# First stage of a two-layer diffusion backbone: adaLN scale and shift made one feature tile at a time

## The chip, the cores and the metric

The kernel runs on one core of a Trainium2 chip. Five engines work beside one another, each through its own instructions in order: TensorE (PE, with its weight loads PEld), VectorE (DVE), ScalarE (ACT), GpSimd (POOL) and SyncE (SP), whose queue issues most of the loads; 16 DMA engines move the data. The metric is the time of one execution on the device in microseconds, as the median of several runs.

## What is computed

The reference is one inference step of two trunk layers over 640 tokens (512 latent and 128 context tokens) of width 1024. Layer 0 mixes with latent attention and neighbourhood attention, layer 1 with grouped-query attention; each is followed by a SwiGLU network. What the change touches is the head of layer 0: the modulation vectors, the first norm and the first projection.

```python
def rms_norm(x, g):
    xf = x.astype(jnp.float32)
    y = xf * lax.rsqrt(jnp.mean(xf * xf, axis=-1, keepdims=True) + RMS_EPS)
    return (y * g.astype(jnp.float32)).astype(x.dtype)

def ada_modulation(cond, w_mod, b_mod):
    m = jax.nn.silu(cond) @ w_mod + b_mod
    return jnp.split(m, 6, axis=-1)

def modulate(h, shift, scale):
    return h * (1.0 + scale) + shift
...
        sh1_p, sc1_p, g1_p, sh2_p, sc2_p, g2_p = ada_modulation(cond_ctx, w_mod[l], b_mod[l])
        sh1_s, sc1_s, g1_s, sh2_s, sc2_s, g2_s = ada_modulation(cond_lat, w_mod[l], b_mod[l])
        hp = modulate(rms_norm(xp, norm_mix[l]), sh1_p, sc1_p)
        hs = modulate(rms_norm(xs, norm_mix[l]), sh1_s, sc1_s)
...
def even_project(h, w_in, q_norm, w_uq, kv_norm, w_ukv):
    b, L, _ = h.shape
    p = h @ w_in
```

## The kernel before, around the change

Everything is kept transposed: features on the 128 partitions, tokens along the free axis. The width of 1024 is eight feature tiles (KT = 8, index k), each 128 x 640 fp32, worked on in two halves of 320 tokens (HALF); the second half holds 192 latent and 128 context tokens, which have different scale and shift, so many instructions of half 1 come as a pair of 192 and 128 columns.

Products in nearly full precision are made of three passes: an operand is split into a high part (rounded to fp32r) and a low part (the rest), and `mm3` (L181) adds high x high, high x low and low x high into one PSUM bank. `unit` (L166) loads a block of weights of 128 x 1024 into a raw buffer (`load`, a ring of three), lets ScalarE make the high part (L171) and VectorE the low part (L172), and puts both into the ring of three weight buffers `wp`.

The first stage in the order of its lines. `Norm` (L193) squares each x tile on ScalarE and adds the squares on VectorE into one accumulator for each half (L202, L205, L206); `rstd` sums the accumulator over the partitions with one fp32 matmul by a matrix of ones and takes the reciprocal root as Ln and Exp on ScalarE (L213, L214). The shift and the scale of two feature tiles at a time are made by `mod0(j)` (L334): `rows`, which is its `part(0)` and `part(1)`, multiplies the two condition columns `scol` with 2 MB of `w_mod` (the tiles mraw) in 16 matmuls of 256 columns, four of which stand in different column strips of the array, and copies the result from its bank to SBUF on ScalarE (modsb, L352); `end` adds the four strips together and turns them with two small matmuls by the selector `sel`, and adds the bias on VectorE (mods, L360). In the trace each fp32 matmul shows as two records, so the 16 of one j are 32 records. `mkgs` (L364) multiplies 1 + scale with the norm's gain (gs, L367). `Mod.make` (L226) then makes one half of one tile: x times gain times reciprocal root on VectorE (h00t, L232), plus the shift on ScalarE, which is the high part (h00h, L236), and the low part on VectorE (h00l, L237).

`first(ks, us)` (L496) does the projection of the tiles ks for three blocks of columns: u = 0 and 1 are the 256 query columns (weights wA0, wA1; banks wA0a to wA1b), u = 2 the rotary columns (weights wA4). Each tile, block and half takes the three matmuls of `mm3`, 144 in all for the eight tiles.

The order of the stage is written out by hand. On SP's queue: the eight x tiles (L487), then 2 MB for j = 0 (`fetch`, L505 to L508, two loads of 1 MB), wA0, 2 MB for j = 1, wA1, wA4, and 4 MB for j = 2 and 3. On TensorE, `run` (L113) chains the pieces: instructions of a piece come behind the last TensorE instruction of the piece before it. The other engines have no such chain; a scheduler orders their instructions by the order of the program and by when their inputs are ready. The list (L530 to L538) is: the sums of squares, rows 0, end 0 and make tiles 0 and 1, rows 1, u = 0 on tiles 0 and 1, end 1 and make tiles 2 and 3, u = 1 and 2 on tiles 0 and 1, rows 2, and so on; at the end all three blocks on tiles 6 and 7.

Behind the stage, wA2 and wA3 are split (L590) and the key-value latent is projected (banks ckv0a to ckv1b), then the values of the neighbourhood heads (nvp), then its queries and keys (nq, nk). The G1 gate vectors are made on VectorE in between (`mod_v`, L557). The four later pairs of shift and scale (SH2, SC2) use the same `mod0` with j = 4 to 7 in pieces much further on (L884).

PSUM has four banks of the kind "m" and four of the kind "y". In the stage wA0a to wA1b are the "y" banks, the two banks of u = 2 are of kind "m", and the sums of squares and the modulation share the other two.

## Time and profile before

| what | us |
|---|---|
| three runs | 1524.39, 1525.30, 1525.52 (median 1525.3) |
| the profiled execution, its own time | 1525.08 |
| its span | 1523.3 |
| granted TensorE clock, mean | 0.994 |

The profile is of one execution. Its page gives the busy time of each engine; the timeline lists instructions in order of time (start, duration, engine, line, operation, output <- input, count; in brackets the idle time before it and what ended it); the window table gives busy times between two points of the span. Matmuls overlap in the pipeline, so the distance between two starts, and not the printed duration, is what one of them costs. Times count from the start of the span.

### The profile page before, as it was taken

The numbers are of one execution on the slowest core, as the hardware profiler recorded it, in microseconds if no ns is written. First come the engines' busy times: TensorE is split into PE (matmuls) and PEld (weight loads), VectorE is DVE, ScalarE is ACT, GpSimd is POOL, SyncE is SP. The second block draws the span as 40 slices with busy tenths as digits, with TensorE's granted clock in tenths as the row PEclk, the third lists the DMA queues.
The fourth block names the chain that finished last, engine by engine and source line by source line (L and its number), as shares of the span: only waits on it lengthen the run. The fifth ranks groups of instructions, "written<-read, shape, count | busy, mean of one in ns | idle before, by whom it ended". The sixth has DMA issues, their size and how long they took to land. (4 is left out here: it accounts for less than half of the span.)

```text
span 1523.3 us, 25525 instructions
## 1 busy us (share of the span) xinstructions
PE 1469.4 (96%) x9894; PEld 1413.1 (93%) x9894; DVE 1133.7 (74%) x2150; ACT 738.3 (48%) x1426; POOL 173.6 (11%) x270
## 2 busy tenths in 40 slices
PE   6999989899999999999999999999999999999997
PEld 4989878889999999999999999989999999999997
DVE  5877778877878888946998878855988888833333
ACT  5446667763745555531124566653745555531221
POOL 0046535320000000000000122210000000000000
PEclk9999999999999999999999999999999999999999
DMA  9543331024164444568764200102154554466211
GB/s 375 194 150 119 114 140 43 14 87 176 46 211 152 163 163 167 183 204 324 231 221 142 91 29 29 56 15 97 52 193 154 174 164 166 138 240 234 84 44 70
DMA packets 73553, 215.08 MB, mean 141 GB/s; under 512 B 8152, under 2 KB 13048, under 8 KB 73048
## 3 DMA queue, kind: packets, MB, share of 16 engines
q1 hardware_dynamic: 71072, 209.04, 40.3%
q10 hardware_dynamic: 1944, 3.48, 0.7%
q8 instruction: 77, 1.26, 0.3%
q0 software_dynamic: 416, 0.93, 0.2%
q14 instruction: 44, 0.36, 0.1%
HBM read 184.96 MB, written 28.47 MB: 140 GB/s over the span
## 5 line engine op out<-in xcount | busy, mean ns | idle before, releaser
L1338 DVE SCALAR_TENSOR_TENSOR junk<-wm,cb 128x1024 bf16<-128x1024 f32 x104 | 126.7, 1218 | 4.6 <-DMA wm<-in_wm 3.9
L62 PE MATMUL gq<-h10h,wgq 128*128 128x320 f32 x256 | 65.8, 316 | 0.0
L246 POOL TENSOR_SCALAR h10h<-h10t,gs,mods 128x320 fp32r<-128x320 f32 x4 | 3.1, 787 | 437.2 <-DVE h10t L240 432.9
L1108 ACT ACTIVATE wY<-s 128x1024 fp32r<-128x1024 f32 x37 | 39.2, 1060 | 28.2 <-PE fg L62 22.8
L1108 ACT ACTIVATE wZ<-s 128x1024 fp32r<-128x1024 f32 x37 | 39.2, 1060 | 24.8 <-PE fd L62 22.9
L1109 DVE TENSOR_TENSOR wZ<-s,wZ 128x1024 fp32r<-128x1024 f32 x37 | 45.3, 1224 | 4.1 <-ACT wZ L1108 0.4
L1177 DVE TENSOR_TENSOR sg<-up,sg 128x640 f32<-128x640 f32 x37 | 30.4, 821 | 21.9 <-ACT sg L1176 21.9
L62 PEld LDWEIGHTS gq<-h10h,wgq 128*128 128x128 f32 x256 | 44.9, 189 | 0.6
L1109 DVE TENSOR_TENSOR wY<-s,wY 128x1024 fp32r<-128x1024 f32 x37 | 45.1, 1218 | 0.3
L62 PE MATMUL fg<-h01q,wgu 128*128 128x320 f32 x192 | 40.3, 316 | 0.9 <-ACT h01q L288 0.5
L1176 ACT ACTIVATE sg<-fg 128x320 f32<-128x320 f32 x37 | 16.2, 438 | 49.3 <-PE fg L62 49.3
L62 PE MATMUL fg<-h11N,wZ 128*128 128x320 f32 x228 | 37.8, 316 | 1.9 <-ACT p L1208 1.9
L62 PE MATMUL gq<-h10l,wgq 128*128 128x320 f32 x128 | 39.5, 308 | 0.0
L1541 ACT ACTIVATE gp<-gs,gb,rq 128x640 f32<-128x640 f32 (+1 forms) x40 | 31.8, 795 | 15.0 <-DVE gb L1540 13.3
L314 DVE SCALAR_TENSOR_TENSOR xr<-fo,mods,xr 128x320 f32<-128x320 f32 (+2 forms) x48 | 19.6, 435 | 25.4 <-PE fo L62 25.3
L1210 ACT ACTIVATE p<-fd 128x320 f32<-128x320 f32 x37 | 16.2, 438 | 45.5 <-PE fd L62 45.5
L62 PEld LDWEIGHTS fg<-h11N,wZ 128*128 128x128 f32 x228 | 35.3, 193 | 2.1 <-ACT p L1208 2.1
L62 PE MATMUL fu<-h11q,wX 128*128 128x320 f32 x228 | 36.8, 310 | 0.0
L62 PE MATMUL fg<-h11q,wX 128*128 128x320 f32 x228 | 36.7, 309 | 0.0
L62 PE MATMUL fg<-h11E,wW 128*128 128x320 f32 x228 | 36.6, 310 | 0.0
L62 PE MATMUL fd<-h11q,wZ 128*128 128x320 f32 x228 | 36.6, 309 | 0.0
L62 PE MATMUL fd<-h11D,wY 128*128 128x320 f32 x228 | 36.4, 308 | 0.0
(3055 smaller groups left out, 5297.2 us busy)
## 6 DMA issues: line engine op xcount, KB each, us to landing
wm<-in_wm SPq DMA_DIRECT2D x48, 512.0 KB, 4.4
mraw<-in_wm SPq DMA_DIRECT2D x8, 1024.0 KB, 13.1
mraw<-in_wm SPq DMA_DIRECT2D x16, 512.0 KB, 3.5
wmv<-in_wm0g SPq DMA_DIRECT2D x8, 512.0 KB, 3.8
wm<-in_wm0g SPq DMA_DIRECT2D x8, 512.0 KB, 5.4
x<-in_xT SPq DMA_DIRECT2D x8, 320.0 KB, 5.1
xr<-in_xT SPq DMA_DIRECT2D x8, 320.0 KB, 6.0
cb<-crs SPq DMA_DIRECT2D x2, 1024.0 KB, 7.6
```

The costliest lines, as they stand in the source:

```text
L62: cls.last = nc.tensor.matmul(*a, **k)
L246: G.tensor_scalar(h[:, c0:c1], t, self.gsl[:, k, 0:1], self.ml[:, self.sh + k, 0:1], ALU.mult, ALU.add)
L314: V.scalar_tensor_tensor(xo[:, c0:c1], ps[:, c0 - o:c1 - o], ml[:, g + n, c:c + 1], xi[:, c0:c1], ALU.mult, ALU.add)
L1108: S.activation(t[:, 0, :], src, AF.Copy)
L1109: V.tensor_tensor(t[:, 1, :], src, f(t[:, 0, :]), ALU.subtract)
L1176: last = S.activation(sg[:, 0:HT], g[:, :HT], AF.Silu, scale=-1.0)
L1177: V.tensor_tensor(sg, up, sg, ALU.mult)
L1210: S.activation(p5, b5[:, :HT], AF.Copy)
L1338: V.scalar_tensor_tensor(junk, raw, 1.0, cb[:, c, :], ALU.mult, ALU.mult, accum_out=mods[l][:, j0 + i, c:c + 1])
L1541: S.activation(dst, src, AF.Exp, bias=nb, scale=rq[:, j:j + 1], accum_out=ll[:, j:j + 1])
```

## The change

- The shift and scale of layer 0's first norm are made for one feature tile at a time. A new array `wm0s` holds, for each tile k, 1 MB: for each of the eight k tiles of w_mod 128 columns of shift and 128 of scale. `mod_k(k)` multiplies it in eight matmuls of 256 columns, in four column strips, and adds the strips with two matmuls by a new selector `sel4` (128 x 2). The scale half is finished and turned into `gs` ahead of the shift half. `wm0` keeps only the four pairs for SH2 and SC2; `MOD0` and the later index of `mod0` follow.
- The squares are summed on TensorE: the squares of tiles 2p and 2p + 1 are added on VectorE, and a matmul by the ones adds the pair into a PSUM bank for each half, eight matmuls in all. In the second half of odd tiles VectorE squares in place of ScalarE.
- wA0 is loaded and split ahead of x. The order of the loads is wA0, x, block 0, block 1, wA1, block 2, wA4, blocks 3 to 7. wA4's two parts get a buffer of their own, so that wA2 can be split before the stage's results are read; wA2's line moves up accordingly.
- The low parts of wA1 and wA4 are made in four instructions of 256 columns each (`parts=4`).
- The list of pieces goes tile by tile: rows(k + 2), u = 1 and 2 on tile k, end and make of tile k + 2, u = 0 on tile k + 1; with a list of its own for the first tiles.

The diff, without the signature of the body and the list of inputs, where `wm0s` is added:

```diff
@@ -38,7 +38,7 @@
 
 SH1, SC1, G1, SH2, SC2, G2 = 0, 8, 16, 24, 32, 40
 
-MOD0 = [(SH1 + j, SC1 + j) for j in (0, 2, 4, 6)] + [(SH2 + j, SC2 + j) for j in (0, 2, 4, 6)]
+MOD0 = [(SH2 + j, SC2 + j) for j in (0, 2, 4, 6)]
 
 MOD0V = list(range(G1, G1 + 8))
 NA_U = 47
...
@@ -141,6 +141,9 @@
     V.memset(sel, 0.0)
     for g in range(4):
         V.tensor_copy(sel[32 * g:32 * g + 32, g // 2 * 2:g // 2 * 2 + 2], ident[32 * g:32 * g + 32, 32 * g:32 * g + 2])
+
+    sel4 = main.tile([P, 2], F32, name="sel4")
+    V.tensor_tensor(sel4, sel[:, 0:2], sel[:, 2:4], ALU.add)
     mods = [main.tile([P, 48, 2], F32, name=f"mods{l}") for l in range(2)]
     gs = [[main.tile([P, 8, 2], F32, name=f"gs{l}{i}") for i in range(2)] for l in range(2)]
 
...
@@ -163,13 +166,16 @@
         nc.sync.dma_start(raw[:, :n], src)
         return raw[:, :n]
 
-    def unit(src, n, name, lo="v", pool=None, bufs=3):
+    def unit(src, n, name, lo="v", pool=None, bufs=3, parts=1):
 
         raw = load(src, n, name + "r")
         t = (pool or wp).tile([P, 2, 1024], F32R, tag="w", bufs=bufs, name=name)
         hi, lw = t[:, 0, :n], t[:, 1, :n]
         S.activation(hi, raw, AF.Copy)
-        (V if lo == "v" else G).tensor_tensor(lw, raw, f(hi), ALU.subtract)
+        m = n // parts
+        for i in range(parts):
+            c = slice(m * i, m * i + m)
+            (V if lo == "v" else G).tensor_tensor(lw[:, c], raw[:, c], f(hi[:, c]), ALU.subtract)
         return hi, lw
 
     def after(inst, fn):
...
@@ -361,6 +367,29 @@
                                 bc2(bmod(0, t, 2)), ALU.add)
         return [part(0), part(1), end]
 
+    def mod_k(k, bk, raw):
+
+        box = []
+
+        def rows():
+            box.append(bk())
+            for j in range(KT):
+                r = slice(32 * (j % 4), 32 * (j % 4) + 32)
+                PE.matmul(box[0][r, :256], scol[:, j, :], raw[:, 256 * j:256 * j + 256], start=j < 4, stop=j > 3,
+                          tile_position=(0, r.start))
+            box.append(tp.tile([P, HT], F32, tag="u", bufs=7, name=f"modsb{k}"))
+            S.activation(box[1][:, :256], box[0][:, :256], AF.Copy)
+
+        def end():
+            psm, sb = box
+            for i in (1, 0):
+                PE.matmul(psm[:, 2 * i:2 * i + 2], sb[:, i * P:(i + 1) * P], sel4, start=True, stop=True)
+            for i, t in ((1, SC1 + k), (0, SH1 + k)):
+                V.tensor_tensor(mods[0][:, t, :], psm[:, 2 * i:2 * i + 2], bc2(bmod(0, t, 1))[:, 0, :], ALU.add)
+                if i == 1:
+                    mkgs(0, 0, k, k + 1)
+        return rows, end
+
     def mkgs(l, i, k0=0, k1=8):
         sc = SC1 if i == 0 else SC2
         n = (V_NMIX if i == 0 else V_NFFN) + 8 * l
...
@@ -480,15 +509,29 @@
         return get
 
 
-    nrm = Norm("n00", D)
+    w3 = [unit(wA[0], 1024, "wA0")]
     x = []
     for k in range(KT):
         xk = ring.tile([P, T], F32, tag="x", name=f"x0_{k}")
         nc.sync.dma_start(xk, xT[:, k, :])
         x.append(xk)
+
+    n00 = [bank(f"n00p{i}") for i in range(2)]
+    sq = {}
     for k in range(KT):
-        for i in range(2):
-            nrm.add(x[k], i)
+        for i, (c0, c1) in enumerate(HALF):
+            sq[k % 2, i] = t = tp.tile([P, HT], F32, tag="u", bufs=7, name=f"n00sq{k}{i}")
+            if i == 0 or k % 2 == 0:
+                S.activation(t, x[k][:, c0:c1], AF.Square)
+            else:
+                V.tensor_tensor(t, x[k][:, c0:c1], x[k][:, c0:c1], ALU.mult)
+            if k % 2:
+                V.tensor_tensor(t, t, sq[0, i], ALU.add)
+                after(PE.last, lambda: PE.matmul(n00[i][:, :HT], ones, t, start=k == 1, stop=k == KT - 1))
+    rs0 = tmp("n00rs")
+    for i, (c0, c1) in enumerate(HALF):
+        S.activation(rs0[:, c0:c1], n00[i][:, :HT], AF.Ln, bias=eps, scale=1.0 / D)
+        S.activation(rs0[:, c0:c1], rs0[:, c0:c1], AF.Exp, scale=-0.5)
     hm = Mod("h00", x, gs[0][0], mods[0], SH1, (range(8), range(8)))
     hh, hl = hm.hh, hm.hl
     pss = [pair(f"wA{u}") for u in range(2)] + [[bank(f"wA2{c}") for c in range(2)]]
...
@@ -502,40 +545,40 @@
     with tc.tile_pool(name="start", bufs=1) as big:
         raws = {}
 
-        def fetch(j):
-            for half in range(2):
-                raws[j, half] = big.tile([P, 2, 1024], F32, tag="mraw", bufs=8, name=f"mraw{j}_{half}")
-                nc.sync.dma_start(raws[j, half], wm0[j, 2 * half:2 * half + 2].rearrange("q p n -> p q n"))
+        def fetch(k):
+            raws[k] = big.tile([P, 2 * D], F32, tag="mraw", bufs=8, name=f"mraw{k}")
+            nc.sync.dma_start(raws[k], wm0s[k])
 
 
         fetch(0)
-        w3 = [unit(wA[0], 1024, "wA0")]
         fetch(1)
-        w3 += [unit(wA[i], 1024, f"wA{i}") for i in (1, 4)]
+        w3.append(unit(wA[1], 1024, "wA1", parts=4))
         fetch(2)
-        fetch(3)
-        m = [mod0(j, lambda j=j: bank(f"mod{j}", "m"), lambda j, half: [raws[j, half][:, q, :] for q in range(2)]) for j in range(4)]
-
-        def made(j):
-
-            m[j][2]()
-            mkgs(0, 0, 2 * j, 2 * j + 2)
-            for k in (2 * j, 2 * j + 1):
+        w3.append(unit(wA[4], 1024, "wA4", pool=big, bufs=1, parts=4))
+        for k in range(3, KT):
+            fetch(k)
+        m = [mod_k(k, lambda k=k: bank(f"mod{k}"), raws[k]) for k in range(KT)]
+
+        def rows(k):
+            return m[k][0]
+
+        def made(k):
+
+            def run():
+                m[k][1]()
                 for i in range(2):
-                    hm.make(i, nrm.rs, k)
-
-        def rows(j):
-            return m[j][:2]
-
-        nrm.rstd(0)
-        run([lambda: nrm.rstd(1)] + rows(0))
-        run([lambda: made(0)] + rows(1))
-        run([lambda: first((0, 1), [0]), lambda: made(1), lambda: first((0, 1), [1, 2])])
-        run(rows(2))
-        run([lambda: first((2, 3), [0]), lambda: made(2), lambda: first((2, 3), [1, 2])])
-        run(rows(3))
-        run([lambda: first((4, 5), [0]), lambda: made(3), lambda: first((4, 5), [1, 2])])
-        run([lambda u=u: first((6, 7), [u]) for u in range(3)])
+                    hm.make(i, rs0, k)
+            return run
+
+        def some(ks, us):
+            return lambda: first(ks, us)
+
+        run([rows(0), made(0), rows(1), made(1), some((0,), [0]), rows(2), some((0,), [1]), made(2), some((1,), [0, 1]), rows(3),
+             some((0, 1), [2]), made(3), some((2,), [0])])
+        for k in range(2, KT):
+            ahead = k + 2 < KT
+            run(([rows(k + 2)] if ahead else []) + [some((k,), [1, 2])] + ([made(k + 2)] if ahead else []) +
+                ([some((k + 1,), [0])] if k + 1 < KT else []))
     sb = ExitStack()
     ab = sb.enter_context(tc.tile_pool(name="ab", bufs=1, reuse_waits="tile"))
 
...
@@ -580,6 +623,7 @@
             for u in range(2):
                 V.scalar_tensor_tensor(ts[u][:, c0:c1], ts[u][:, c0:c1], vcol(vn + u), rs[:, c0:c1], ALU.mult, ALU.mult)
 
+    w2 = [unit(wA[2], 1024, "wA2")]
     cq, nrq = lowrank("cq", pss)
     tk = load(tabK, T, "tabK")
     ka, kb = tmp("kra"), tmp("krb")
...
@@ -587,7 +631,7 @@
         ps = pss[2][c]
         V.tensor_tensor(ka[0:32, c0:c1], ps[0:32, :HT], tk[0:32, c0:c1], ALU.mult)
         done = V.tensor_tensor(kb[0:32, c0:c1], ps[32:64, :HT], tk[32:64, c0:c1], ALU.mult)
-    w2 = [unit(wA[i], 1024, f"wA{i}") for i in (2, 3)]
+    w2.append(unit(wA[3], 1024, "wA3"))
     for i in range(2):
         after(done, lambda: mod_v(i, raw0[i]))
     pss = [pair(f"ckv{u}") for u in range(2)]
...
@@ -881,7 +925,7 @@
             pieces.update(named("q", na_q(p + 1) if r == 0 else na_k(p + 1)))
         for n, at in enumerate(M_AT):
             if h == at:
-                pieces.update(named("m", mod0(4 + n, lambda n=n: bank(f"mod{4 + n}", "y"), mod_raw)))
+                pieces.update(named("m", mod0(n, lambda n=n: bank(f"modb{n}", "y"), mod_raw)))
         if h == 7:
             pieces.update(named("k", k_pieces(0, ybank)))
             pieces.update(named("u", q_pieces(0, ybank, lambda c: ring.tile([P, T], F32R, tag="h" + c, name=f"mq{c}0"),
...
@@ -1681,7 +1725,9 @@
     d["crow"] = np.concatenate([a["c"][0], a["c_ctx"]])[None]
     t = a["w_mod"][0].reshape(D, 48, P)
     t = np.concatenate([t[:, i:i + 2] for j in MOD0 for i in j], 1)
-    d["wm0"] = t.reshape(4, 2, P, 8, 512).transpose(3, 0, 2, 1, 4).reshape(8, 4, P, 1024)
+    d["wm0"] = t.reshape(4, 2, P, 4, 512).transpose(3, 0, 2, 1, 4).reshape(4, 4, P, 1024)
+    t = a["w_mod"][0][:, :2 * D].reshape(KT, P, 2, KT, P)
+    d["wm0s"] = t.transpose(3, 1, 0, 2, 4).reshape(KT, P, 2 * D)
     d["wm0g1"] = a["w_mod"][0].T.reshape(48, P, D)[MOD0V]
     d["wm0g"] = a["w_mod"][0][:, 5 * D:].T.reshape(8, P, D)
     d["wm1"] = a["w_mod"][1].T.reshape(48, P, D)
```

4 lines of the change are left out of this document (2 added, 2 removed).

## The prediction

> **What bounds the kernel now.** I read the page first, for the share of each engine.
>
> ```profile
> span 1523.3 us, 25525 instructions
> ...
> PE 1469.4 (96%) x9894; PEld 1413.1 (93%) x9894; DVE 1133.7 (74%) x2150; ACT 738.3 (48%) x1426; POOL 173.6 (11%) x270
> ```
>
> TensorE is busy for 96% of the span, so the change can only pay where TensorE is not yet running, or where its work shrinks. Second view: the busy times by stage, cut where TensorE passes from one job to the next (sum of squares from 13.44, first projection at 24.41, wA2's projection at 53.11, the first neighbourhood scores at 110.66). Columns: PE, PEld, DVE, ACT, POOL busy us, granted clock, DMA share, GB/s.
>
> ```profile
> 13.44:24.41 10.97, 9.45 (x72) 4.10 (x72) 3.96 (x11) 4.63 (x9) 0.00 (x0) 0.93 1.03 411
> 24.41:53.11 28.70, 28.33 (x224) 25.27 (x221) 20.56 (x57) 15.41 (x36) 0.00 (x0) 0.97 0.75 285
> 53.11:110.66 57.55, 57.55 (x322) 52.21 (x321) 48.20 (x84) 23.44 (x44) 16.79 (x32) 1.00 0.56 181
> ```
>
> From 53.11 to 110.66 TensorE has no gap at all, and neither VectorE nor the DMAs are at their limit there. So a stage that ends X earlier moves what follows by X, and I price only the work up to 53.11. Third view: the timeline of TensorE before its first projection.
>
> ```profile
> 13.44 2.50 PE L62 MATMUL n00p<-n00acc,ones 128*128 128x320 f32 x4 [8.30 <-DVE n00acc L206]
> 15.87 3.64 PE L62 MATMUL mod<-mraw,scol 128*32 128x256 f32 x32
> 20.02 0.61 PE L62 MATMUL mod<-sel,modsb 128*128 128x4 f32 x4 [0.50 <-ACT modsb L352]
> 20.56 1.07 PE L62 MATMUL mod<-mraw,scol 128*32 128x256 f32 x16
> 22.64 1.84 PE L62 MATMUL mod<-mraw,scol 128*32 128x256 f32 x16 [1.02 <-DMA mraw<-in_wm]
> 24.41 0.64 PE L62 MATMUL wA0a<-h00h,wA 128*128 128x320 f32 x1
> ```
>
> The first projection (24.41) stands behind the second modulation block, whose second half had to wait for its DMA (22.64). That wait, and the 8.30 us for the sum of squares, are what the change goes after. The same rows show a second thing: 16 modulation records take 1.07 us at 20.56 but 1.84 us at 22.64. The clock column of the same stretches (PE busy, granted clock, DMA share, GB/s) says why:
>
> ```profile
> 22.64:24.41 1.77, 1.77 (x16) 0.55 1.03 410
> 24.41:26.18 1.77, 1.77 (x10) 0.50 1.03 410
> 26.18:28.20 2.02, 2.02 (x15) 0.99 1.03 410
> ```
>
> TensorE fell to half clock after the gaps at 19.5 to 22.6 and was back at full clock at 26.18. (The 32 records at 15.87 ran at half speed too.)
>
> **When the data arrives.** The order of the loads on SP's queue sets this.
>
> ```profile
> 7.86 0.34 SPq L163 DMA_DIRECT2D wA0r<-in_wA  x1
> ...
> 10.30 0.34 SPq L163 DMA_DIRECT2D wA1r<-in_wA  x1
> ...
> mraw<-in_wm SPq DMA_DIRECT2D x8, 1024.0 KB, 13.1
> ...
> wA0r<-in_wA SPq DMA_DIRECT2D x1, 512.0 KB, 9.6
> wA1r<-in_wA SPq DMA_DIRECT2D x1, 512.0 KB, 13.6
> ```
>
> wA0 lands at 7.86 + 9.6 = 17.46, wA1 at 10.30 + 13.6 = 23.90. Between them lie two mraw blocks and wA1 itself, 2.62 MB in 6.44 us: 0.407 MB/us, or 2.58 us for 1024 KB, 1.29 for 512 KB. Counting back, x has landed at 17.46 - 1.29 - 2 x 2.58 = 11.0. The change moves no byte away; it puts wA0 ahead of x (x done at 12.3) and needs two blocks fewer ahead of wA1: block 0 at 14.9, block 1 at 17.5, wA1 at 18.8, block 2 at 21.3, wA4 at 22.6, then one block each 2.58 us, the last at 35.5. Behind them on SP stand wA2, tabK, wA3 and wmv as before; wA2's buffer comes free earlier, but its load is still behind block 7. Packets of wm0s are longer (8 KB a partition in one run); as the DMA share already reads 1.03 at 411 GB/s I give that nothing.
>
> **The opening.** The sum of squares moves from a chain of VectorE adds to 8 fp32 matmuls in 4 pairs. Two such (4 records) took 2.50 us above, at half clock. The first pair waits for x's second tile (each 320 KB is 0.81 us, so 12.3 - 6 x 0.81 = 7.4) and for a square and an add: four 320-column VectorE instructions take 1.61 (a row below), so 0.8 for the two, an estimate, and TensorE starts at about 8.3. The idle 8.30 us of before covers the first three pairs; without it they would cost 6 x 1.25. The fourth waits for x's last tile, 12.3 + 0.8, and for TensorE. Half clock lasted from 13.44 to at least 19.51 before, 6 us; if it does so again from 8.3, three pairs are done at 15.2 to 15.8 and the fourth, mostly at full clock, at 16.0 to 16.9. At full clock throughout it is 14.4, at half throughout 18.3. I take **16.0**: full clock came at the latest at 20.56, and the fourth pair alone then takes 1.25. What is queued behind these waits is little: the square tiles now live until TensorE has read them, in seven buffers of which a pair takes four, so ScalarE's later squares may stall a little behind TensorE, and nothing but wA0's split (next rows) goes ahead of them on ScalarE, while x is on its way.
>
> ```profile
> 16.54 0.47 ACT L214 ACTIVATE n00rs<-n00rs 128x320 f32<-128x320 f32 x1
> ...
> 19.86 1.05 ACT L171 ACTIVATE wA<-wA0r 128x1024 fp32r<-128x1024 f32 x1
> ...
> 21.77 0.91 ACT L236 ACTIVATE h00h<-h00t,mods 128x320 fp32r<-128x320 f32 x2 [0.86 <-DVE h00t L232]
> ...
> 21.98 1.22 DVE L172 TENSOR_TENSOR wA<-wA0r,wA 128x1024 fp32r<-128x1024 f32 x1
> ```
>
> The reciprocal root ended at 17.01, 1.07 after its last matmul (13.44 + 2.50); it now ends at 17.1. Block 0: 16 records from 16.0, 0.93 us at full clock and 1.82 at half (half of 1.86 and of 3.64), to 16.9 or 17.8. From the end of the records (19.51) to the end of the selector (20.56) it took 1.05: selector 0 done at 18.0 to 18.9. Block 1 is there (17.5): to 18.9 or 20.7; its copy and selector, 1.05 again: 20.0 to 21.8. The first part of tile 0 is ready 22.2 - 20.56 = 1.7 us after its own selector, by 20.6 at the latest, so it is mostly the second selector that ends last. First projection at **20.8**, against 24.41: 3.6 us earlier.
>
> **What TensorE then has to do.**
>
> ```profile
> 31.78 0.31 PE L62 MATMUL wA<-h00h,wA 128*128 128x320 f32 x1
> ...
> 32.02 1.93 PE L62 MATMUL mod<-mraw,scol 128*32 128x256 f32 x32
> 33.88 0.41 PE L62 MATMUL wA0a<-h00h,wA 128*128 128x320 f32 x1
> ...
> 35.60 0.31 PE L62 MATMUL wA0b<-h00h,wA 128*128 128x320 f32 x1
> 35.75 0.50 PE L62 MATMUL mod<-sel,modsb 128*128 128x4 f32 x4
> 36.11 0.39 PE L62 MATMUL wA1a<-h00h,wA 128*128 128x320 f32 x1
> ...
> 53.11 0.31 PE L62 MATMUL ckv0a<-h00h,wA 128*128 128x320 f32 x1
> ...
> 56.63 0.31 PE L62 MATMUL ckv0b<-h00h,wA 128*128 128x320 f32 x1
> ```
>
> One 320-column matmul: 24 from 53.11 to 56.63, 0.147 us. A modulation block of 32 records: 33.88 - 32.02 = 1.86, and 0.09 to enter (32.02 - 31.78 - 0.147). A selector: 36.11 - 35.60 - 0.147 = 0.36. Before, from 24.41: 144 matmuls 21.1, two blocks 3.9, three selectors 1.1, in all 26.1; the other 2.6 of 28.70 are half clock (1.77 at 0.50, so 0.9) and waits. After, from 20.8: the same 21.1; six blocks of half the size, 6 x (0.93 + 0.09) = 6.1; six selectors, each as dear as one for two tiles, 2.2: **29.4**. The finer grain moves one more tile's worth of modulation behind the start and doubles the selectors: 3.3 us more behind a start that is 3.6 earlier.
>
> The Trainium skill speaks to this (TensorEngine Tiling (Array Packing), Key Properties): changing the tiling mode drains the array. The rows agree, with 0.09 us at entry; by the rule alone, without a size, the sum would only be larger.
>
> **What is late next.** VectorE makes each tile.
>
> ```profile
> 36.35 0.23 DVE L360 TENSOR_TENSOR mods<-mod,vec 128x4 f32<-128x4 f32 x2 [1.34 <-PE mod L62]
> 36.62 0.16 DVE L367 SCALAR_TENSOR_TENSOR gs<-mods,vec 128x4 f32<-128x4 f32 x1
> 36.81 1.61 DVE L232 SCALAR_TENSOR_TENSOR h00t<-x,gs,n00rs 128x320 f32<-128x320 f32 x4
> 38.34 1.60 DVE L237 SCALAR_TENSOR_TENSOR h00l<-h00t,mods,h00h 128x320 fp32r<-128x320 f32 x4
> 39.86 0.67 DVE L232 SCALAR_TENSOR_TENSOR h00t<-x,gs,n00rs 128x192 f32<-128x192 f32 x2
> 40.79 0.68 DVE L237 SCALAR_TENSOR_TENSOR h00l<-h00t,mods,h00h 128x192 fp32r<-128x192 f32 x2 [0.26 <-ACT h00h L236]
> ```
>
> From 36.35 to 41.47 it makes two tiles; the 12 large instructions take 4.4 without the idle 0.26, so 2.2 a tile, and the three small ones 0.46, now paid for each tile: 2.7. With selector 0 at 18.2, tile 0 is made by 20.9, a quarter of wA1's low part (1.22 / 4 = 0.3) follows, tile 1 by 23.9. TensorE meanwhile: wA0 on tile 0 to 21.7, block 2 (landed 21.3) to 22.7, wA1 on tile 0 to 23.6, selector to 23.9. It then needs tile 1: no wait, or 0.9 if all of wA1's low part runs first, and 0.5 more where ScalarE copies wA1 (1.05) ahead of tile 0's high part. I take 0.8. Quartering the low part is worth that 0.9 and costs three more VectorE starts off the path. After that TensorE needs 18 x 0.147 + 1.02 + 0.36 = 4.0 us a tile against 2.7 on VectorE and 2.58 on the DMA; block 7 is wanted at about 43 and lands at 35.5. Neither comes last again. The half clock: between nothing and 3.4 us of work at double price (+1.7); I take 0.7, near the 0.9 of before, as the opening keeps its gaps around the selectors.
>
> wA2's split moves from the end of the stage into it (1.05 on ScalarE, 1.22 on VectorE, beside TensorE): there was no gap at 53.11 that it could close, and with an earlier end it keeps one from opening. wA4 leaves the ring of three weight buffers, so wA3 waits for wA0's release at the last tile, some 7 us ahead of its use (ckv1a stands 48 matmuls behind ckv0a). The second half of wm0, the new selector sel4 and the index of the later mod0 pieces change no work.
>
> **Sum.** 20.8 + 29.4 + 0.8 + 0.7 = **51.7** against 53.11: 1.4 us less. The profiled execution took 1525.08 (span 1523.3, 1.8 around it), 0.2 under the median of 1525.3; 1525.08 - 1.4 = **1523.7**. Its ends: 20.0 + 29.4 = 49.4, -3.7 (1521.4); 21.8 + 29.4 + 1.4 + 1.7 = 54.3, +1.2 (1526.3). TensorE's waits after 110.66 can shift by a microsecond either way, as VectorE's and SP's orders are drawn up anew.
>
> **The rivals.**
> First, **faster still**: the clock is full from the squares on (TensorE works almost without a break from 8.3 on), the selectors follow their copies closely, and the quarters slip between the tiles: 49.4 to 50.0; 1521.6. For it: 20.56 shows full clock after 6 us of such work. Against it: the fall to 0.55 only 2 us later.
>
> Second, **nothing gained**: the first projection still stands behind block 1 and its selector, and the scheduler lets VectorE do wA1 whole before tile 0's low part. Start 21.8, wait 1.4, clock 0.7: 53.3; 1525.3. For it: at 21.98 VectorE did run a whole split ahead of the first low part (23.11).
>
> Third, **slower**: the many short gaps of the opening keep TensorE at half clock past 26.18, for one more stretch as long as that from 22.64 to 26.18 (3.54), to 29.7. Place: the projections from 21.8 to 29.7. Price: half of 7.9, 4.0 in place of 0.7: 21.8 + 29.4 + 1.4 + 4.0 = 56.6, +3.5; 1528.6. It decides when of some 3 us near 24 only about half is TensorE work; 19.51 to 22.64, with 0.61 and 1.07 of 3.1 us, was such a stretch. The Trainium skill (TensorE: Matmul & The Clock Gate, Part 1) gives the rule: half rate is the default, and a busy window of some 3.4 us lifts it, at a phase that no kernel sets. By that rule alone the phase decides between the first and third cases; the trace agrees with both speeds.
>
> **How the numbers follow.** Forecast 0.35; faster still 0.31; nothing gained 0.17; slower 0.17. 0.2% is 3.05 us (about what a measurement of this kernel tells from no change): under 1522.25 is faster, over 1528.35 slower. The first rival, and 0.02 of the forecast, lie below: 0.33. The third rival counts as slower, 0.17, and 0.50 lies between. Range 1520.7 to 1527.4: it takes in the bounds of the sum, most of the first rival with a microsecond of later waits, and part of the third. The forecast's own range is 1521.4 to 1526.3.
>
> **What would show it.** Right: first projection near 20.8 and ckv0a near 51.7; six blocks of 16 records between projections, each with its own selector; the sum of squares ended by 16.0; no DMA wait for mraw after 22. Wrong: the first projection after 22.5; a clock of 0.5 beyond 26.5; TensorE waiting for the low parts more than 1.5 us in all; or a gap at ckv0a. If ckv0a moves and the end of the span does not follow it, the assumption that the dense stretch passes the shift on is what failed.

## The result and the profile after

The changed kernel took 1534.31 us (median of 5 runs, 1531.06 to 1535.3) against 1525.52 for the kernel before beside it: a ratio of 1.0048, 95% interval 1.0036 to 1.0061. Two repeats gave 1.0034 (1.0020 to 1.0049) and 1.0047 (1.0022 to 1.0072). It is slower, by 4.5 to 8.8 us; the forecast was 1523.7 and the range ended at 1527.4. The page of the profiled execution (1534.31):

```profile
span 1532.5 us, 25600 instructions
...
PE 1478.5 (96%) x9922; PEld 1419.4 (93%) x9922; DVE 1134.1 (74%) x2167; ACT 735.0 (48%) x1426; POOL 173.6 (11%) x270
```

TensorE is busy 9.1 us longer than before (1469.4), and the span is 9.2 longer, but the one is not the cause of the other: 4.3 of the 9.1 lie ahead of 16 us, where TensorE now sums squares (busy 7.46 in place of 3.14) in time that was idle before, and matmuls at half clock count as busy for longer. The windows at the cuts of before (columns as there):

```profile
13.44:24.41 10.97, 8.60 (x60) 5.68 (x62) 5.71 (x19) 5.87 (x14) 0.00 (x0) 0.86 1.02 426
24.41:53.11 28.70, 28.70 (x239) 23.55 (x236) 20.02 (x65) 11.31 (x28) 0.00 (x0) 0.94 0.53 217
53.11:110.66 57.55, 56.08 (x314) 50.47 (x313) 47.06 (x81) 24.86 (x48) 13.66 (x26) 1.00 0.62 202
```

The stage has no TensorE gap from 24.41 on, but a lower clock (0.94, before 0.97); and the stretch that had no gap before has one now: 56.08 of 57.55. TensorE's timeline, cut to the rows that answer to those of before:

```profile
10.56 5.95 PE L62 MATMUL n00p<-n00sq,ones 128*128 128x320 f32 x14 [0.47 <-DVE n00sq L529]
16.44 1.07 PE L62 MATMUL mod<-mraw,scol 128*32 128x256 f32 x16
18.28 0.61 PE L62 MATMUL mod<-sel,modsb 128*128 128x2 f32 x4 [0.77 <-ACT modsb L381]
18.82 1.07 PE L62 MATMUL mod<-mraw,scol 128*32 128x256 f32 x16
21.49 1.01 PE L62 MATMUL mod<-sel,modsb 128*128 128x2 f32 x4 [1.60 <-ACT modsb L381]
22.36 0.61 PE L62 MATMUL wA0a<-h00h,wA 128*128 128x320 f32 x1
...
33.15 0.50 PE L62 MATMUL mod<-sel,modsb 128*128 128x2 f32 x4
33.52 0.39 PE L62 MATMUL wA0a<-h00h,wA 128*128 128x320 f32 x1
33.74 0.31 PE L62 MATMUL wA0a<-h00l,wA 128*128 128x320 f32 x1
...
34.56 1.07 PE L62 MATMUL mod<-mraw,scol 128*32 128x256 f32 x16
35.56 0.42 PE L62 MATMUL wA1a<-h00h,wA 128*128 128x320 f32 x1
35.82 0.31 PE L62 MATMUL wA1a<-h00l,wA 128*128 128x320 f32 x1
...
37.43 0.50 PE L62 MATMUL mod<-sel,modsb 128*128 128x2 f32 x4
...
55.95 0.31 PE L62 MATMUL ckv0a<-h00h,wA 128*128 128x320 f32 x1
```

The first projection starts at 22.36, 2.05 earlier than before, and ckv0a at 55.95, 2.84 **later**. Where the difference grows is seen from the same matmuls in several executions of the two kernels (start in us; half clock is 24 us x 2 x (1 - granted clock) of the window 16 to 40):

| | before | before, repeat | changed | repeat | repeat |
|---|---|---|---|---|---|
| half clock in 16 to 40 | 3.4 | 0 | 6.7 | 3.4 | 6.7 |
| first projection | 24.41 | 23.82 | 22.36 | 21.31 | 22.16 |
| ckv0a | 53.11 | 51.83 | 55.95 | 55.24 | 55.50 |
| first scores | 110.66 | 109.38 | 115.23 | 114.33 | 114.89 |
| first fg (layer-0 network) | 391.06 | 391.91 | 396.44 | 394.73 | 395.89 |
| first gq (layer 1) | 864.76 | 864.48 | 874.23 | 869.61 | 871.77 |
| span | 1523.3 | 1521.0 | 1532.5 | 1527.8 | 1528.1 |

Three places, then: the stage itself (to ckv0a), the stretch from ckv0a to the first scores (57.55 in both profiles of before, 59.1 to 59.4 here), and the network of layer 0 between fg and gq (472.6 and 473.7 before, 474.9 to 477.8 here). Between the first scores and fg the five differ by up to 2.1 us; each of them has two or three stretches of half clock of 3.4 us there, which cost some 1.7 each.

**Place one: the opening.** ScalarE's timeline shows why selector 1 waited 1.60:

```profile
17.48 0.47 ACT L534 ACTIVATE n00rs<-n00rs 128x320 f32<-128x320 f32 x1
17.86 0.36 ACT L381 ACTIVATE modsb<-mod 128x256 f32<-128x256 f32 x1
19.97 1.20 ACT L242 ACTIVATE h00h<-h00t,mods 128x320 fp32r<-128x320 f32 x3 [1.75 <-DVE h00t L238]
21.07 0.36 ACT L381 ACTIVATE modsb<-mod 128x256 f32<-128x256 f32 x1
```

Block 1's records had ended at 18.82 + 1.07 = 19.89, but its copy (21.07) stands behind the high part of tile 0, for which ScalarE waited 1.75. TensorE idled around both selectors, and its clock fell (windows of 2 us):

```profile
18.00:20.00 2.00, 1.61 (x20) 0.94 (x20) 0.97 (x5) 0.25 (x2) 0.00 (x0) 1.00 1.00 422
20.00:22.00 2.00, 0.51 (x3) 0.51 (x3) 1.67 (x5) 2.00 (x5) 0.00 (x0) 0.82 1.04 430
22.00:24.00 2.00, 2.00 (x9) 1.91 (x8) 1.36 (x6) 0.79 (x2) 0.00 (x0) 0.50 1.01 426
...
26.00:28.00 2.00, 2.00 (x12) 1.90 (x8) 0.63 (x2) 1.60 (x3) 0.00 (x0) 0.50 1.01 426
```

The lower clock holds from 21.3 to 28.1. The same gaps don't always have this effect at this place: in the first repeat TensorE has the same gap of 1.60 ahead of selector 1 (at 20.84) and worked 2.40 us of 18 to 22, but its clock fell only at 26.5, behind one more gap of 1.14.

**Place two: nq.** TensorE's and ScalarE's waits, and SP's own queue, of the changed kernel:

```profile
PE nq L62 <- ACT nvf L671: 1.5, 1, 1.5
...
SPq L771 <- POOL bm L777: 11.8, 2, 7.8
...
ACT wnk L174 <- DMA wnk0r<-in_wNA: 8.9, 1, 8.9
...
91.79 0.56 SPq L771 DMA_DIRECT2D gt<-in_rpbp  x1
92.44 0.54 SPq L166 DMA_DIRECT2D wnk0r<-in_wNA  x1
```

and SP's queue of the kernel before:

```profile
80.86 0.33 SPq L163 DMA_DIRECT2D wnk0r<-in_wNA  x1
89.48 0.56 SPq L727 DMA_DIRECT2D gt<-in_rpbp  x1
```

The load of the second head's bias table (gt, L771) waits for a buffer that GpSimd still reads (the SPq row above). In the changed kernel the scheduler put it ahead of the first key weights wnk0r, so these are issued at 92.44 in place of 80.86; ScalarE waits 8.9 for them, in order, and so copies the values (nvf) late, whose bank nq needs.

**Place three: the layer-0 network.** VectorE's and TensorE's waits between 530 and 650, changed kernel, the longest of them:

```profile
DVE junk L1382 <- DMA wm<-in_wm: 4.7, 4, 1.9
DVE s L1240 <- DMA wg_20r<-in_wFI: 2.1, 1, 2.1
...
PE fg L62 <- ACT u L1258: 1.7, 4, 0.6
```

and before, where TensorE has no wait in this window:

```profile
DVE s L1196 <- DMA wg_15r<-in_wFI: 2.0, 1, 2.0
...
DVE junk L1338 <- DMA wm<-in_wm: 0.7, 2, 0.4
```

All waits of VectorE for wg are 10.8 in this window against 6.5 before. The loads of wm land later, too: the median from issue to landing of the seven in this window, changed kernel first, then before:

```profile
wm<-in_wm SPq DMA_DIRECT2D x7, 512.0 KB, 5.6
...
wm<-in_wm SPq DMA_DIRECT2D x7, 512.0 KB, 4.6
```

### The profile page after: what moved, and what is told of

Same layout as the page of the kernel before. It is cut to its first block, busy times and chain, and to the rows that moved or that the text cites. A ratio compares the mean times of both kernels' runs of the same rounds, so it can differ in the third digit from the quotient of the medians.

```text
span 1532.5 us, 25600 instructions
## 1 busy us (share of the span) xinstructions
PE 1478.5 (96%) x9922; PEld 1419.4 (93%) x9922; DVE 1134.1 (74%) x2167; ACT 735.0 (48%) x1426; POOL 173.6 (11%) x270
## 4 chain that ended last, share of the span: by engine, by line
PE 65%; DVE 16%; DMA 8%; ACT 6%; issue 4%; POOL 0%; DVEq 0%; ACTq 0%; SPq 0%; POOLq 0%
PE fg L62 13%; PE fo L62 7%; PE fd L62 6%; PE fu L62 3%; PE gq L62 3%; DVE junk L1382 3%; PE gs L62 2%; DMA wm<-in_wm 2%; PE nk L62 2%; PE go L62 2%; PE nq L62 1%; PE ms L62 1%; DVE junkv L600 1%; PE gt L66 1%; PE fo_2b L62 1%
## 5 line engine op out<-in xcount | busy, mean ns | idle before, releaser
L62 PE MATMUL fg<-h01C,wY 128*128 128x320 f32 x216 | 35.1, 311 | 1.7 <-ACT u L1258 1.7
L62 PE MATMUL fg<-h11C,wY 128*128 128x320 f32 x228 | 36.4, 308 | 0.0
```

Of the source, the lines that this page charges most:

```text
L62: cls.last = nc.tensor.matmul(*a, **k)
```

## The experiments

Ratios are to runs of the kernel before on the same chip, with 95% intervals. Single runs of the kernel before lie between 1520.87 and 1534.25, so a ratio is known to 0.001 to 0.002 only; the starts in a profile tell more of a single place than the times do. Much of this spread is half clock, wherever it falls in the span: over the 135 single runs of the kernel before that stand beside the experiments, the mean granted clock lies between 0.988 and 0.996, and the time is longer where it is lower (correlation -0.74).

**The kernel before as it was, and the changed one.** No edit.

> The changed kernel once more, unedited, beside the same runs of the kernel before: the yardstick for the edits, and a second profile. Theory (of the 9.2 us at the end of its first profile, the 2.8 at ckv0a and the 1.5 at nq belong to the kernel, but the four short waits between 548 and 640 and the clock's phase do not): ratio 1.002 to 1.004, ckv0a at 55 to 56, the wait at nq again, the waits between 548 and 640 gone or fewer. Rival (those waits follow from the lateness): they are there again, about 4 us, and the ratio is 1.005.

> The kernel before once more, for a second profile of the loads between 530 and 650. So far the changed kernel and most of its variants show VectorE waiting 9 to 13 us there for loads of wg and 3.4 to 4.8 for wm, and TensorE up to 3.1 behind it; the kernel before and three variants of it show 5 to 6.5 and under 0.7, and TensorE none. Theory (which of the two it is belongs to the kernel): the lower waits again. Rival (it falls differently from one execution to the next): the higher waits.

> The changed kernel a third time: by the theory that the waits between 530 and 650 belong to the kernel, VectorE again waits 9 to 12 us for wg and TensorE 0.5 to 2.5; by the rival, under 7 and none. Time 1.002 to 1.005 of the kernel before.

Measured: the starts are in the table above. The two repeats of the changed kernel have 1.0034 and 1.0047; the repeat of the kernel before is one profiled run, of 1522.76. In that order, VectorE's waits for wg and wm between 530 and 650 are: 10.5 and 3.7 (changed), 6.2 and 0.8 (before), 9.9 and 4.9 (changed). The clock in the opening does change from one execution of a kernel to the next; nq's wait (1.3 to 1.6) and the waits in the layer-0 network do not. My theory for the first repeat, that these last are chance, fell.

**Fill the gaps of the opening.**

```diff
+        def fill(n):
+            def go():
+                for _ in range(n):
+                    PE.matmul(pss[2][0][:, :P], ones, ones, start=True, stop=True)
+            return go
-        run([rows(0), made(0), rows(1), made(1), some((0,), [0]), ...
+        run([rows(0), fill(3), made(0), rows(1), fill(7), made(1), fill(3), some((0,), [0]), ...
```

> The changed kernel with 13 extra fp32 matmuls of 128 columns on data that nothing reads: 3 behind block 0, 7 behind block 1, 3 behind selector 1, so that TensorE is not idle around the first two selectors. Theory (the gaps there throttle the clock, and half clock over 21.3 to 28.1 costs about half of the 6 us of work that falls into it): clock 1.0 from 18 to 30, ckv0a at 52.7 to 53.5 in place of 55.95, and 2 to 3 us off the time of the changed kernel (1531 to 1532). Rival (the late start is selectors and blocks, the clock is a side show): ckv0a between 55.3 and 56.5, time unchanged.

> The changed kernel with 13 extra matmuls once more: one of the two changed variants that showed the lower waits (5.2 and 0.4). Theory (belongs to the kernel): the lower waits again. Rival (differs by execution): the higher waits, 9 us and more for wg.

Measured: 1.0017 (1.0004 to 1.0030), where the changed kernel has 1.0034 to 1.0048. No half clock between 16 and 40 in either profile. The first projection is at 23.16 and 21.73, ckv0a at 54.85 and 53.43: between the two lie 31.69 and 31.70, where the three profiles of the changed kernel have 33.34 to 33.93. So half clock is a cause of the late ckv0a. In the first profile the gain at ckv0a was only 1.1, less than expected, since the first projection was 0.8 later: block 0 began 0.5 later (16.98), behind squares that took longer, and the fill outlasts the gaps by 0.3. That profile also shows that an early ckv0a alone does not make a fast run: TensorE still waited 1.9 at nq (2.1 in the second), had half clock again at 104 (granted clock 0.66 in 103 to 108), and reached the first scores at 116.15, 0.9 later than the first profile of the changed kernel. It is the slowest of its twelve runs, 1531.45 against a median of 1527.86. The second reached them at 113.30. The lower waits in the layer-0 network came in both profiles (wg 5.2 and 5.2), so the gain in the time is not the clock's alone.

**The same in the kernel before.**

```diff
         nrm.rstd(0)
-        run([lambda: nrm.rstd(1)] + rows(0))
-        run([lambda: made(0)] + rows(1))
+        run([lambda: nrm.rstd(1)] + rows(0) + [fill(2)])
+        run([lambda: made(0), rows(1)[0], fill(5), rows(1)[1]])
```

> The kernel before with seven extra matmuls of 128 columns that nothing reads, two behind block 0 and five inside block 1 ahead of its second half, which waits for its DMA. Theory (gaps around the selectors throttle the clock in the kernel before too, though shorter): clock 1.0 from 16 to 30, first projection within 0.5 of 24.41, ckv0a 0.5 to 1.5 earlier, time 0 to 2 less than the kernel before. Rival (the half clock at 22.8 has nothing to do with these gaps): a half-clock stretch in the opening again.

> The kernel before with seven extra matmuls in the opening once more, on whichever chip: 0.997 to 0.999 of the kernel before, full clock from 16 to 30, the lower waits between 530 and 650. If the gain was chance: ratio 1.000 and over.

Measured: 0.9981 (0.9969 to 0.9992) and 0.9989 (0.9978 to 0.9999), 1522.7 both times: **faster than both kernels**, by little, but with both intervals under 1. Its TensorE timeline:

```profile
18.49 0.71 PE L62 MATMUL wA<-ones 128*128 128x128 f32 x4
19.08 0.61 PE L62 MATMUL mod<-sel,modsb 128*128 128x4 f32 x4
20.37 1.07 PE L62 MATMUL mod<-mraw,scol 128*32 128x256 f32 x16 [0.69 <-DMA mraw<-in_wm]
21.37 1.38 PE L62 MATMUL wA<-ones 128*128 128x128 f32 x10
22.92 1.07 PE L62 MATMUL mod<-mraw,scol 128*32 128x256 f32 x16 [0.17 <-DMA mraw<-in_wm]
```

Block 1's second half takes 1.07 where it took 1.84 before, and ckv0a starts at 52.36 and 52.58. Over 16 to 40 both profiles have a clock of 1.00. The repeat of the kernel before, which had no half clock there without any fill, reached ckv0a earlier still (51.83): the fill costs some 0.5 to 0.8 itself and pays in the executions that would have had half clock.

**One load moved.**

```diff
# load() keeps each transfer in loads, by name
...
-        nc.sync.dma_start(gt.rearrange("p a b -> p (a b)"), src)
+        after(loads["wnk0r"] if h == 1 else None,
+              lambda: nc.sync.dma_start(gt.rearrange("p a b -> p (a b)"), src))
```

> The changed kernel with one load moved: the bias table gt of the second neighbourhood head is issued behind the first key weights wnk0r on SP, as it stands in the kernel before. Theory (wnk0r, late behind gt, which itself waits for its buffer, holds up ScalarE, and so nvf and TensorE at nq): wnk0r issued at about 84 in place of 92.4, the wait at nq gone, shift at 111 about +2.8 in place of +4.4, time 1.5 us less than the changed kernel. Rival (the wait at nq has another cause, or something else ends last): shift at 111 stays over +4.

Measured: 1.0019 (1.0005 to 1.0033). SP's queue:

```profile
88.92 0.33 SPq L168 DMA_DIRECT2D wnk0r<-in_wNA  x1
91.04 0.33 SPq L168 DMA_DIRECT2D wnq1r<-in_wNA  x1
91.42 0.56 SPq L773 DMA_DIRECT2D gt<-in_rpbp  x1
```

wnk0r is issued at 88.92 (not 84, it still waits for a buffer), early enough: no wait at nq, and from ckv0a to the first scores it takes 112.86 - 55.31 = 57.55, as before to the digit. This place is shown.

**A pure delay in the kernel before.**

```diff
     pss = [pair(f"ckv{u}") for u in range(2)]
+    for _ in range(6):
+        PE.matmul(pss[0][0][:, :HT], ones, hm.x[7][:, :HT], start=True, stop=True)
```

> The kernel before with six fp32 matmuls of 320 columns, whose results are overwritten, just ahead of ckv0a: a pure delay of TensorE, 6 x 0.62 = 3.7 us, at the point where the change delivers its 2.8. Theory A (a delay is passed on at its own size, and the further 6.4 us come from what the change does to the orders): shift 3.7 at 111 and 3 to 5 at the end, 1528 to 1530. Theory B (what follows is so close to its loads that any delay of this size meets the same waits): the shift grows by 4 us or more in the layer-0 network between 548 and 640, as in the changed kernel, 1532 to 1535.

Measured: 1.0010 (0.9998 to 1.0023). Against the repeat of before, which like this execution had no half clock in the opening, ckv0a is 3.3 later (55.13), the first scores 3.6 (113.01), the end of TensorE's work 3.7; no wait at nq, wg 6.2. The places agree with theory A: lateness is passed on at its own size and brings neither of the later waits. The time agrees less well, 1.5 us over the kernel before where 3 to 5 were expected.

**The edit at the stage's end, alone and undone.** Alone in the kernel before:

```diff
-        w3 += [unit(wA[i], 1024, f"wA{i}") for i in (1, 4)]
+        w3 += [unit(wA[1], 1024, "wA1"), unit(wA[4], 1024, "wA4", pool=big, bufs=1)]
...
+    w2 = [unit(wA[2], 1024, "wA2")]
     cq, nrq = lowrank("cq", pss)
...
-    w2 = [unit(wA[i], 1024, f"wA{i}") for i in (2, 3)]
+    w2.append(unit(wA[3], 1024, "wA3"))
```

> The kernel before with nothing but the edit at the stage's end: wA4's parts in a buffer of their own, wA2's load and split ahead of the reading of the results. Theory (the loss comes from the opening and from what a later stage meets behind it; the weight loads for the first keys stay ahead of the second bias load on SP here): ckv0a at 53.1 plus or minus 0.3, no wait at nq, 1524 to 1527, same as before. Rival (moving wA2 upsets SP's and ScalarE's orders by itself): a wait of over 1 us between 55 and 111, and 1527 to 1530.

> The changed kernel without the edit at the stage's end: wA4 back in the ring of three, wA2 split behind the reading of the results, as in the kernel before. Theory (wA2's earlier split reorders SP and ScalarE and opens waits at nvp3b and nq, as it did alone): 1.5 to 3 us less than the changed kernel, no wait of over 0.5 us at nvp or nq; ckv0a itself no earlier than 55.5. Rival (wA2's early split is what the end of the stage needs, or the order of the bias load behind wnk0r alone decides): a gap of 0.5 us or more at ckv0a, or the wait at nq still there, and no gain.

Measured: alone 1.0033 (1.0017 to 1.0049). ckv0a came at 52.17, earlier than expected, but the first scores at 113.30, 2.6 later than before; TensorE's waits between 60 and 111:

```profile
PE nvp3b L62 <- ACT ckvr L572: 1.9, 1, 1.9
PE nq L62 <- ACT nvf L628: 1.1, 1, 1.1
```

My theory fell: by itself the edit costs the kernel before nearly as much as the whole change does. Undoing it in the changed kernel (the inverse of this diff) won nothing, 1.0031 (1.0018 to 1.0044): there the waits at nvp and nq are gone, but the matmuls of cqp wait 1.6 and ckv0a 0.7 in their place, as its rival said, and ckv0a comes at 57.76. So the edit changes which waits there are: of no effect on the time that can be told in the changed kernel, harmful alone.

**The opening's order, the grain, x first, the squares.** Four versions of the changed kernel:

```diff
# blocks 0 and 1 ahead of the selectors
+        run([rows(0), rows(1), made(0), made(1), some((0,), [0]), ...
# later blocks in pairs
+        for k in range(2, KT, 2):
+            run(([rows(k + 2), rows(k + 3)] if ahead else []) + [some((k,), [1])] +
+                ([made(k + 2), made(k + 3)] if ahead else []) + [some((k,), [2]), some((k + 1,), [0, 1, 2])] + ...
# wA0 behind block 0
         fetch(0)
+        w3 = [unit(wA[0], 1024, "wA0")]
# the sum of squares as before
+    nrm = Norm("n00", D)
+            nrm.add(x[k], i)
```

> The changed kernel with block 1's rows ahead of selector 0 in TensorE's list, so that both copies modsb go ahead of tile 0's high part on ScalarE. Theory (selector 1, and with it the first projection, stood behind ScalarE's high part of tile 0, 1.2 us and a wait of 1.75 for it): selector 1 by 20.0 in place of 21.49, selector 0 at about 19 in place of 18.3, first projection at 21.0 to 21.6 in place of 22.36, ckv0a 0.8 to 1.4 earlier. Rival (VectorE, which makes tile 0 behind selector 0, ends last): first projection no earlier than 22.2.

> The changed kernel with blocks 4 and 5, and 6 and 7, and their selectors, put beside one another in TensorE's list: the same matmuls, but two entries into the strip mode and two groups of selectors where there were four each. Theory (a block costs 1.2 and a selector 0.45 beside projections because each entry and exit costs some 0.3 and 0.35 beyond the records' own time): 0.9 to 1.4 us less between the first projection and ckv0a, at equal clock. Rival (the cost lies in the records themselves, or VectorE falls behind when it gets two tiles at once): under 0.4 us less, or waits for the low parts of 0.5 us and more.

> The changed kernel with wA0 loaded and split behind block 0 in place of ahead of x. Theory (wA0 ahead of x makes x 1.2 to 1.3 later, and with it the sum of squares, which ended at 16.5 against 15.9 before): sum of squares ended at 15.2 to 15.4, first projection at equal order 0.5 to 1.2 earlier, unless wA0's split (1.05 on ScalarE, 1.22 on VectorE) takes that back between 16 and 20. Rival (the split in the busy place costs as much as x's delay): first projection at 22.0 to 23.0, no gain.

> The changed kernel with the sum of squares as before: squares added on VectorE, two matmuls by the ones at the end. Theory (the squares on TensorE end when their last pair does, 16.5, about when two matmuls behind VectorE's last add would end, and they keep TensorE busy ahead of the opening): sum of squares ended between 16.0 and 17.5, first projection within 0.7 of the changed kernel's, more half clock in the opening. Rival (the squares are what brings the opening forward): first projection over 1 us later than 22.4.

Measured, in that order: 1.0046, 1.0036, 1.0022, 1.0038 (intervals of 0.0010 to 0.0019 to each side).
Rows first: selector 1 is through by 19.7, the first projection at 20.77 (1.6 earlier, more than expected), yet ckv0a at 57.54, 1.6 later where 0.8 to 1.4 earlier were expected. TensorE waited 1.1 ahead of its first projection and 0.2 and 0.8 behind it for tile 0's parts, and had half clock for 10.1 us in 16 to 40. Waits and clock together took twice the gain.
Pairs: 8.23 for two tiles (block to block, 33.60 to 41.83) against 8.54 (selector to selector, 33.15 to 41.69); from block 4 to ckv0a 20.75 against 21.39, 0.64 less for the two pairs. A miss: the expected 0.9 was not reached, and ckv1a then waited 1.0 for wA's low part, as the rival had it.
x first: the squares ended at 15.3, 1.2 earlier, the first projection at 21.85, only 0.5 earlier, since wA0's split now stood on ScalarE from 16.27 and on VectorE from 17.34, ahead of modsb and mods. Both forecasts in part.
Squares as before: they end at 17.05 and the first projection is at 23.61, 1.25 later, with 3.4 us of half clock and not more than the changed kernel. The rival holds: the squares on TensorE do bring the opening forward. They account for the 0.5 by which block 0 starts later (16.98); the rest is a longer wait for selector 1's copy (2.54 in place of 1.60).

**Together.** Rows first, five fill matmuls, pairs, load moved, and the low parts of wA1 and wA4 on GpSimd (`lo="g"`); then the load moved with seven fill matmuls, without and with pairs, in the changed kernel's own order.

> The changed kernel with what the runs so far point to: blocks 0 and 1 ahead of the selectors, five extra matmuls of 128 columns that nothing reads behind them, later blocks in pairs, the low parts of wA1 and wA4 in one instruction each on GpSimd in place of VectorE, and the second bias load behind wnk0r on SP. Theory (late selector, half clock, entries of the strip mode, and the load order are what cost the time): first projection at 20.8 to 21.3, clock 1.0 from 16 on, ckv0a at 50.5 to 52.5, no wait at nq; 1521 to 1524, 1 to 4 less than the kernel before. Rival (the gain at ckv0a is again given back by later waits, as with the wait for wA's low part in the paired version): ckv0a as said, shift at the first scores 0 or more, 1525 to 1528.

> The changed kernel with the second bias load behind wnk0r on SP and seven extra matmuls of 128 columns that nothing reads (2 behind block 0, 4 behind block 1, 1 behind selector 1). Theory (of the 4.5 us that the changed kernel loses, about 1.5 are the load order, some 2.5 half clock, and the rest TensorE work that the finer grain adds, 0.38 us a tile over six tiles, less what the earlier start gives): clock 1.0 from 16 to 30, ckv0a at 52.7 to 54, first scores at 110.3 to 112, and 1525 to 1527, level with the kernel before. Rival (the loss has a further part in later stages that neither edit touches): ckv0a and the first scores as said, time 1528 and over.

> The same with the blocks from tile 4 on and their selectors in pairs. Theory: 0.3 us less for each of the two pairs up to ckv0a, 0.4 to 0.9 in all, unless wA2's or wA3's low part comes late again (1.0 at ckv1a in the paired version): first scores 0 to 0.9 earlier than without pairs. Rival (what TensorE saves is lost again in a wait for VectorE): first scores within 0.3.

Measured: 1.0020 (1.0008 to 1.0031), 1.0024 (1.0013 to 1.0035), 1.0008 (0.9995 to 1.0022).
The first failed at a new place. Timelines of VectorE, GpSimd and TensorE there:

```profile
19.64 3.26 DVE L240 SCALAR_TENSOR_TENSOR h00t<-x,gs,n00rs 128x320 f32<-128x320 f32 x3
...
20.07 2.35 POOL L180 TENSOR_TENSOR wA<-wA1r,wA 128x1024 fp32r<-128x1024 f32 x1 [18.76 <-ACT wA L176]
...
23.47 0.42 PE L62 MATMUL wA0b<-h00h,wA 128*128 128x320 f32 x1 [2.22 <-ACT h00h L244]
```

In the changed kernel the same three VectorE instructions took

```profile
19.38 1.15 DVE L238 SCALAR_TENSOR_TENSOR h00t<-x,gs,n00rs 128x320 f32<-128x320 f32 x3
```

which is 2.1 less: VectorE stood still while GpSimd subtracted. It happened again at GpSimd's second subtraction, to an instruction of VectorE that takes 0.16 elsewhere:

```profile
29.63 1.89 DVE L398 SCALAR_TENSOR_TENSOR gs<-mods,vec 128x2 f32<-128x2 f32 x1
...
29.11 2.40 POOL L180 TENSOR_TENSOR wA<-wA4r,wA 128x1024 fp32r<-128x1024 f32 x1 [6.68 <-ACT wA L176]
```

The Trainium skill (SBUF — State Buffer, SBUF: two separate sides) has it as a lock on a pair of ports, which VectorE needs for two operands from SBUF and which is held for a whole instruction; the rows agree.
TensorE's gap of 2.22 was not filled, half clock of 3.4 us followed, and ckv0a came at 56.15.
The other two have full clock, ckv0a at 54.82 and 53.89, up to 0.8 later than expected, and 57.55 from there to the first scores (112.37 and 111.44): no wait at nq. But both show the longest waits of all in the layer-0 network (wg 12.6 and 12.3, wm 4.4 and 4.8, TensorE 2.8 and 3.1): the rival of the first, a further loss in later stages, was right. The version with pairs is 0.93 earlier at the first scores; 0.29 of this lies ahead of the first projection (22.27 against 22.55), so the pairs gave 0.64, as above. Neither beats the kernel before; the version with pairs is level with it.

## Why the prediction was wrong, step by step

By its own sum (20.8 + 29.4 + 0.8 + 0.7 = 51.7), with what the first profile measured:

| term | predicted | measured | how |
|---|---|---|---|
| first projection | 20.8 (20.0 to 21.8) | 22.36 | 21.31 and 22.16 in the repeats |
| TensorE work behind it | 29.4 | 31.3 | filled repeat, full clock: 53.43 - 21.73 - 0.4 of wait |
| VectorE late | 0.8 | 0 | no wait for a low part from 22.36 on |
| half clock | 0.7 (0 to 1.7) | 2.3 | 55.95 - 22.36 - 31.3 |
| ckv0a | 51.7 | 55.95 | sum |

- **First projection.** The step that failed is "its copy and selector, 1.05 again" for block 1. It took block 1's copy as free to run when the rows end. ScalarE works in order, and tile 0's high part, which waits for VectorE, was ahead: 18.82 + 1.07 to 22.36 took 2.47. The sum of squares (16.5, forecast 16.0 to 16.9) and selector 0 (18.9, forecast 18.0 to 18.9) were right. With the copy ahead, 20.77 was measured.
- **TensorE's work.** The count ("six blocks of half the size", "six selectors, each as dear as one for two tiles") was right in kind and mis-sized: a tile takes 4.27 (33.15 to 37.43), 2.64 of it for 18 matmuls, so 1.63 for block and selector against 1.38 forecast; six times 0.25 is 1.5 of the missing 1.9, and 0.4 stay unexplained. The 0.25 lie mostly in what the forecast had at nothing, the way out: the first matmul behind a block takes 0.26 (35.56 to 35.82) and behind a selector 0.22 (33.52 to 33.74) in place of 0.147, and the block itself 1.00 in place of 0.93. The bigger fact was in the forecast: the grain adds 3.3 us behind a start that came 2 earlier, not 3.6.
- **What VectorE makes.** The quarters and the split of wA1 cost nothing on the path, and no load of mraw came late: TensorE waits for none in the changed kernel. In rows first, where VectorE again ran wA1's four quarters ahead of the low part of tile 0, TensorE waited 0.8: quarters don't slip in between by themselves.
- **Half clock.** The third rival named the mechanism and its place, with half clock to 29.7 at a price of 4.0 (measured: to 28.1, and 2.3), but I gave it 0.17, and 0.7 to the sum. All nine profiles of changed kernels without fill had half clock between 16 and 40 (3.4, 6.7 or 10.1 us); of four of the kernel before and its unfilled variants two had 3.4 and two none. It was the likely case. What could have told me is that the change puts a second selector, with idle time around it, ahead of the first projection: 20 to 22 holds 0.51 us of TensorE work. But the share of work does not decide it, as that rival's criterion (about half of some 3 us) had it: the repeat of the kernel before kept full clock with half of 18 to 24 idle,

```profile
18.00:24.00 6.00, 3.06 (x41) 1.61 (x38) 4.51 (x13) 3.19 (x6) 0.00 (x0) 1.00 1.03 412
```

  and in the first execution of that kernel the same matmuls met half clock. What decides between two executions no run here shows. The Trainium skill's rule (TensorE: Matmul & The Clock Gate, Part 1), a free-running window of some 3.4 us, fits the lengths; its advice to avoid idle gaps of over some 3 us (Why this matters for your kernels) would not have warned here, where the longest gap between 16.44 and 21.49 was 1.60.
- **"The dense stretch passes the shift on."** This assumption failed, as the prediction said it might ("if ckv0a moves and the end of the span does not follow it"). It is true of a delay (the delay experiment) and false of this change, which also redrew SP's order. "Behind them on SP stand wA2, tabK, wA3 and wmv as before" was wrong: wnv0 went ahead of wmv, and gt ahead of wnk0r. That is 1.5 to 1.8 us between ckv0a and the first scores, and moving one load gave it back. I had allowed a microsecond either way behind 110.66 and none ahead of it.
- **The layer-0 network.** Not foreseen, 1.8 to 4.7 us over the mean of the two profiles of before, and not settled. It isn't lateness, nor the order in which the instructions of SP, VectorE or ScalarE stand there: the version with 13 fill matmuls has the changed kernel's order on these engines from tile 2 on, and the lower waits in two profiles of two, while the changed kernel has the higher ones in three of three. Lower (wg 3.5 to 6.5): before, its three variants, the version with 13 fill matmuls, and the one with the squares as before. Higher (9.4 to 12.6): all others. One more sign goes with this in all twenty profiles: the seven loads of wm between 530 and 650 take 3.7 to 4.6 from issue to landing (median) in the lower ones and 5.2 to 6.0 in the higher ones, while over the whole span the median of all 48 such loads is 3.8 to 4.5 in both. So the loads themselves land later there; whether that is the cause or itself follows from something else, and why it is so in one kernel and not in the other, stays open.

In sum, the three profiles of the changed kernel against the two of before, on average: 3.1 later at ckv0a, of which some 2 are half clock (5.6 us of it against 1.7) and the rest the finer grain less what the earlier start gives; 1.7 more to the first scores, by the load order; and 3.1 more between fg and gq, whose cause is open. The spans differ by 7.3.

## What to carry to other kernels

Splitting a stage finer paid here only for the first piece: count what each further piece costs at its entry and exit, and subtract it from the earlier start before anything else. A copy that a TensorE step waits for goes ahead of work on the same in-order engine that itself waits, and an edit at one place is followed through the queues that a scheduler draws up anew, load by load, until they are the same again. Short gaps that lie close together on TensorE may be worth filling with matmuls that nothing reads: seven of them took 1.5 to 2.9 us off the kernel before, by the medians of two comparisons.

## What the runs showed of the hardware that was not expected

- Half clock came in the changed kernel with no TensorE gap over 1.60 us from 16 on, in lengths of 3.4 and 6.7 us within 16 to 40 (10.1 in the variant with rows first), and differed between executions of one kernel (before: 3.4 and none). Extra matmuls in the gaps removed it in six profiles of seven; in the seventh another gap, of 2.22, was left open.
- The clock column misses the start. It reads 1.00 for the kernel before here,

```profile
16.00:18.00 2.00, 2.00 (x20) 0.87 (x23) 0.00 (x0) 0.98 (x2) 0.00 (x0) 1.00 1.04 414
```

  where 32 records took 3.64 (15.87) that take 1.93 at 32.02. Durations of equal instructions are the surer sign.
- A GpSimd subtraction of 2.35 us held up VectorE instructions with two operands from SBUF for about 2.1 us, on the path; a second one, of 2.40, made an instruction of 0.16 last 1.89.
- A change in the first 55 us moved waits for loads at 530 to 650, in the same way in each of the two or three profiles of a kernel.
